# Six small experts of a mixture of experts: three products of 32 to 56 columns instead of two with high and low halves side by side, and one bias operation less

## The chip, the core and the metric

The kernel runs on one core of a Trainium2 chip. The metric is the device time of one execution in microseconds (us). The engines are named as in the profile: PE (TensorE, matrix products; PEld is its weight load), DVE (VectorE), ACT (ScalarE), POOL (GpSimd) and SP (SyncE, which here only issues transfers).

## The reference

One layer of a diffusion trunk on 1024 tokens of width 1024: a token-mixing half (windowed attention and a long convolution) and then a mixture of experts, the only part that the change touches. Cut to what matters:

```python
logits = xt @ router_w + router_b              # 1024 tokens, 32 experts
top_vals, top_idx = lax.top_k(logits, 4)
gate = jax.nn.softmax(top_vals, axis=-1)
# for every expert e, on the tokens tok that chose it, with their gates wt
hb = x[tok] @ w1[e] + b1[e]                    # 1024 -> 2048
glu, lin = jnp.split(hb, 2, axis=-1)
glu = jnp.minimum(glu, 7.0); lin = jnp.clip(lin, -7.0, 7.0)
act = glu * jax.nn.sigmoid(1.702 * glu) * (lin + 1.0)
yb = act @ w2[e] + b2[e]                       # 1024 -> 1024
acc = acc.at[tok].add(yb * wt[:, None])
```

All is float32, and each expert has 12 MB of weights.

## The kernel before

**Precision.** A float32 product is made of float16 ones: each operand is split into a high and a low half, and three passes are added in PSUM: high weight by high value, high weight by low value, low weight by high value. The weights of the experts come from HBM as float32 in 384 pieces of 1 MB (`raw`, line 305, five buffers). Each piece is split in two halves of 128x1024: ACT makes the high half `wh` (line 315) and DVE the low half `wl` (line 317).

**Experts by size.** The experts are sorted by how many tokens chose them, and the expert of rank r gets a fixed number of columns, `CAPS[r]`: 416, 384, 304, 256 and so on down to 56, 48, 32, 32, 32, 32. An expert is worked off in eight units. Units 0 to 3 take two pieces of w1 each (gate and linear part) and make 256 columns of the hidden layer, units 4 to 7 take one piece of w2 each.

**Order of the experts.** `plan` (line 74) interleaves two lanes: lane 0 takes the experts from the largest downward, lane 1 from the smallest upward. At each step it compares two running sums, the estimated product time and the estimated transfer time, and takes the next unit from lane 0 when products are not ahead by more than `SLACK`, else from lane 1. The estimate of an expert's product time is `pecost` (line 72). The framework's scheduler then sets the order on each engine from the program so written.

**Ahead of an expert** its tokens are fetched (`prep_`): DVE makes one-hot tables `S` (line 254), PE multiplies them with the token table (line 262, the index product), DVE turns the result into addresses (`gi`, line 264), POOL issues an indirect transfer that gathers up to 128 rows of 4 KB (line 277), and PE transposes the rows (line 286), which ACT copies to `xT` (line 287).

**Small experts before.** Experts with `C<=CCAT`, that is 56, 48 and four times 32 columns, take another way through `mm3`: their high and low values lie side by side, so that one product of 2C columns with the high weight does the first two passes, and a second of C columns with the low weight adds the third:

```python
if C<=CCAT:
    nc.tensor.matmul(ps_,wh,x[k],start=k==0,stop=False); nc.tensor.matmul(ps_[:,0],wl,x[k][:,0],start=False,stop=k==7)
    continue
for a,b in ((wh,x[0][k]),(wh,x[1][k]),(wl,x[0][k])):
    nc.tensor.matmul(ps_,a,b,start=n==0,stop=n==23); n+=1
```

The sum then lies in PSUM in two parts, and DVE adds them: with four operations more in a unit of w1 (line 396) and two more for each of the eight output blocks (line 420).

**Biases.** The 24 rows of biases of an expert are transposed by PE (line 364) and taken from PSUM by three small DVE operations (lines 366 to 368), which scale the two halves of b1 by 64, add 64 to the second one, and multiply b2 with the output gate.

Of the kernel before, what the change touches and what calls it, by code (L numbers as in the profile page):

```python
# [13 lines left out]
F32 = mybir.dt.float32  # L14
# [5 lines left out]
ALU = mybir.AluOpType  # L20
# [45 lines left out]
D=1024; T=1024; NE=32; NT=8  # L66
CAPS=[416,384,304,256,240,208,200,192,168,152,152,144,144,128,120,120,112,112,112,104,96,88,80,80,72,64,56,48,32,32,32,32]
DMAC,FLOOR,SLACK,PE0=33.7,22.0,10.0,10.0
CCAT=56
HOLD=[]; LMAX=152; HQ=1  # L70
def mmc(N): return max(FLOOR,0.4217*N+2.3)
def pecost(C): return (0.192*(mmc(2*C)+mmc(C)) if C<=CCAT else 0.576*mmc(C))+2.0*-(-C//128)
def dmacost(C): return DMAC+2.1*-(-C//128)
# [21 lines left out]
class Moe:  # L95
    def __init__(s,nc,tc,A,rows,accD,es):
        s.nc,s.tc,s.A,s.rows,s.accD,s.es=nc,tc,A,rows,accD,es
        s.cp=es.enter_context(tc.tile_pool(name="mc",bufs=1))
        nc,cp=s.nc,s.cp
        s.idf=cp.tile([128,128],F32,name="idf"); make_identity(nc,s.idf)  # L100
        s.idh=cp.tile([128,128],F16,name="idh"); nc.vector.tensor_copy(s.idh,s.idf)
        jp=cp.tile([128,128],I32,name="jp"); nc.gpsimd.iota(jp,pattern=[[1,128]],base=0,channel_multiplier=-1)
        s.tri=cp.tile([128,128],F16,name="tri"); nc.vector.tensor_scalar(s.tri,jp,0.0,None,op0=ALU.is_gt)
        s.ones=cp.tile([128,128],F16,name="ones"); nc.vector.memset(s.ones,1.0)
        s.iof=cp.tile([128,NE],F32,name="iof"); nc.gpsimd.iota(s.iof,pattern=[[1,NE]],base=0,channel_multiplier=0,allow_small_or_imprecise_dtypes=True)
        s.io16=cp.tile([128,512],F16,name="io16"); nc.gpsimd.iota(s.io16,pattern=[[1,512]],base=0,channel_multiplier=0,allow_small_or_imprecise_dtypes=True)
        s.pcol=cp.tile([128,1],F32,name="pcol"); nc.gpsimd.iota(s.pcol,pattern=[[0,1]],base=0,channel_multiplier=1,allow_small_or_imprecise_dtypes=True)
        s.dum=cp.tile([128,2],F32,name="dum")
        nc.vector.tensor_scalar(s.dum[:,0:1],s.pcol,1024.0,None,op0=ALU.add)
        nc.vector.tensor_scalar(s.dum[:,1:2],s.pcol,-1.0,-1024.0,op0=ALU.mult,op1=ALU.add)  # L110
        s.mx=cp.tile([128,NT,8],F32,name="mx"); s.mi=cp.tile([128,NT,8],U32,name="mi")
        s.oh=cp.tile([128,NT,4,NE],F16,name="oh"); s.idx=cp.tile([128,NT,4],F32,name="ridx"); s.A16=cp.tile([128,NT,NE],F16,name="A16")
        s.M=cp.tile([128,NT,NE,4],F16,name="M")
# [225 lines left out]
    def mm3(s,ps_,w,c,x,C):  # L339
        nc=s.nc; n=0  # L340
        for k in range(8):
            wh=w[0][:,k,c*128:(c+1)*128]; wl=w[1][:,k,c*128:(c+1)*128]
            if C<=CCAT:
                nc.tensor.matmul(ps_,wh,x[k],start=k==0,stop=False); nc.tensor.matmul(ps_[:,0],wl,x[k][:,0],start=False,stop=k==7)  # L344
# [12 lines left out]
    def expert_(s,C,p,reg,xT,chunks):  # L357
        nc,wk,ps,A=s.nc,s.wk,s.ps,s.A
        e=reg()
        T=lambda dt,name,bufs: wk.tile([128,PMAX[p]],dt,name=name+str(p),bufs=bufs)[:,:C]  # L360
        br=s.brs.pop(reg,None)
        if br is None: br=s.bias_load(e)
        pb=ps.tile([128,512],F32,name="tp",bufs=2)[:,:24]
        nc.tensor.transpose(pb,br,s.idf[:24,:24])
        bc=wk.tile([128,24],F32,name="bc",bufs=4)
        nc.vector.tensor_scalar(bc[:,0:8],pb[:,0:8],64.0,None,op0=ALU.mult)
        nc.vector.tensor_scalar(bc[:,8:16],pb[:,8:16],64.0,64.0,op0=ALU.mult,op1=ALU.add)
        nc.vector.tensor_tensor(bc[:,16:24],pb[:,16:24],s.g2c,op=ALU.mult)
        cat=C<=CCAT
        x=[xT[:,:,k,:C] for k in range(8)] if cat else [[xT[:,q,k,:C] for k in range(8)] for q in range(2)]  # L370
        ah,al=[],[]
        for u in range(4):

            wg=s.jget(); wl=s.jget()
            nb=2 if C<=256 else 1
            for c0 in range(0,2,nb):
                if cat:
                    t=ps.tile([128,4,2,64],F32,name="acc",bufs=4); pg,pl=t[:,0:2,:,:C],t[:,2:4,:,:C]
                elif C<=128:
                    t=ps.tile([128,4,128],F32,name="acc",bufs=4); pg,pl=t[:,0:2,:C],t[:,2:4,:C]  # L380
                else:
                    pg=ps.tile([128,nb,512//nb],F32,name="acc",bufs=4)[:,:,:C]; pl=ps.tile([128,nb,512//nb],F32,name="acc",bufs=4)[:,:,:C]
                for j in range(nb): s.mm3(pg[:,j],wg,c0+j,x,C)
                for j in range(nb): s.mm3(pl[:,j],wl,c0+j,x,C)
                if c0+nb==2: s.jahead(s.ahead)
                T2=lambda dt,name,bufs: wk.tile([128,max(2*PMAX[p],4*CCAT) if PMAX[p]<=256 else 512],dt,name=name+str(p),bufs=bufs)[:,:nb*C].rearrange("p (j c) -> p j c",j=nb)
                g=T2(F32,"sg",2); l=T2(F32,"sl",2); sg=T2(F32,"ss",1)
                for j in range(nb):
                    f=u*2+c0+j
                    if cat:  # L390
                        nc.vector.tensor_scalar(g[:,j],pg[:,j,0],bc[:,f:f+1],None,op0=ALU.add); nc.vector.tensor_scalar(l[:,j],pl[:,j,0],bc[:,8+f:9+f],None,op0=ALU.add)
                        continue
                    nc.vector.tensor_scalar(g[:,j],pg[:,j],bc[:,f:f+1],448.0,op0=ALU.add,op1=ALU.min)  # L393
                    nc.vector.tensor_scalar(l[:,j],pl[:,j],bc[:,8+f:9+f],512.0,op0=ALU.add,op1=ALU.min)  # L394
                if cat:
                    nc.vector.tensor_tensor(g,g,pg[:,:,1],op=ALU.add); nc.vector.tensor_scalar(g,g,448.0,None,op0=ALU.min); nc.vector.tensor_tensor(l,l,pl[:,:,1],op=ALU.add); nc.vector.tensor_scalar(l,l,512.0,None,op0=ALU.min)
                nc.scalar.activation(sg,g,AF.Silu,scale=1.702/64)
                nc.vector.scalar_tensor_tensor(l,l,-384.0,sg,op0=ALU.max,op1=ALU.mult)
                if cat:
                    hl=wk.tile([128,max(2*min(PMAX[p],256),4*CCAT)],F16,name="ah%d"%p,bufs=s.nact(p,nb))[:,:4*C].rearrange("p (j q c) -> p j q c",j=2,q=2); h,lo=hl[:,:,0],hl[:,:,1]  # L400
                else: h=T2(F16,"ah",s.nact(p,nb)); lo=T2(F16,"al",s.nact(p,nb))
                nc.scalar.activation(h,l,AF.Copy,scale=HSC)
                nc.vector.scalar_tensor_tensor(lo,l,HSC,h,op0=ALU.mult,op1=ALU.subtract)  # L403
                for j in range(nb):
                    if cat: ah.append(hl[:,j])
                    else: ah.append(h[:,j]); al.append(lo[:,j])
            yield
        yT=[]
        for u in range(4):

            w=s.jget()
            for c in range(2):
                m=u*2+c
                py=ps.tile([128,512],F32,name="acc",bufs=4)
                py=py[:,:2*C].rearrange("p (q c) -> p q c",q=2) if cat else py[:,:C]
                s.mm3(py,w,c,ah if cat else (ah,al),C)
                if c==1: s.jahead(s.ahead)
                y=T(F32,"yT",8)
                if cat:
                    nc.vector.tensor_copy(y,py[:,0]); nc.vector.tensor_tensor(y,y,py[:,1],op=ALU.add); py=y  # L420
                nc.scalar.activation(y,py,AF.Identity,bias=bc[:,16+m:17+m],scale=s.g2s[:,m:m+1])  # L421
                yT.append(y)
            yield
        s.tail.append(s.rows_out(C,chunks,yT))
        yield
# [943 lines left out]
```

## Time and profile before

| what | value |
|---|---|
| median of 3 runs | 2408.18 us (2398.25 to 2410.37) |
| the profiled execution's own time | 2412.69 us |
| its span in the trace | 2410.9 us |
| PE busy in the span | 2199.2 us (91%) |
| DVE busy in the span | 2053.8 us (85%) |
| ACT busy in the span | 1399.8 us (58%) |
| moved by DMA | 594.17 MB, mean 246 GB/s |

The experts fill the time from about 1047 us to about 2347 us. Shares are averages over the whole execution; the first part of the span is another computation with other limits. Durations of PE's products overlap, since they are pipelined: the pace of a run of products is read from the chain of waits, where a piece stands with its count and its length. The same holds for short DVE operations: the next one starts before the one ahead of it has ended.

### The profile page before, as it was taken

The page shows a single profiled execution, that of the slowest core. Times are in us where ns is not written, and L with a number is a line of the kernel's source. Part 1 is how long each engine was busy: PE and PEld are TensorE (multiplying, and loading weights), DVE is VectorE, ACT ScalarE, POOL GpSimd, SP SyncE. Part 2 cuts the span into 40 slices and gives each one's busy share as a digit, 9 for nine tenths or more (in the row PEclk, how much of TensorE's full clock was granted, in tenths as well). Part 3 has the DMA queues.
Part 4 walks back from the last instruction along what each step waited for, and adds up shares of the span by engine and source line. Part 5 has one row for each costly group of instructions (what it writes and reads, how often), then busy time and mean ns, then how long its engine had stood idle before and what let it go on. Part 6 is the DMA issues. An engine that isn't in the chain of part 4 may idle for free.

```text
span 2410.9 us, 59658 instructions
## 1 busy us (share of the span) xinstructions
PE 2199.2 (91%) x24732; PEld 1659.4 (69%) x24753; DVE 2053.8 (85%) x3767; ACT 1399.8 (58%) x2069; POOL 287.6 (12%) x176
## 2 busy tenths in 40 slices
PE   6899989999898999669999999998989999999991
PEld 4566565545454544346666778997989999999991
DVE  6776898798768858969989999988999999999985
ACT  3522335222236411356877778886878878788881
POOL 0000001000000000002031311212030221211110
PEclk9899999999779999779999999999999999999995
DMA  9424644555314233288999999999999999999984
GB/s 300 127 97 166 194 149 132 170 181 169 94 18 144 84 121 139 89 275 280 337 316 303 328 323 348 356 352 320 333 332 350 359 351 354 351 356 368 360 273 159
DMA packets 520011, 594.17 MB, mean 246 GB/s; under 512 B 16708, under 2 KB 472332, under 8 KB 519350
## 3 DMA queue, kind: packets, MB, share of 16 engines
q1 hardware_dynamic: 493048, 508.27, 62.6%
q0 software_dynamic: 13152, 43.69, 7.1%
q10 hardware_dynamic: 13534, 38.35, 4.7%
q8 instruction: 195, 3.19, 0.5%
q14 instruction: 82, 0.67, 0.1%
HBM read 532.95 MB, written 57.29 MB: 245 GB/s over the span
## 4 chain that ended last, share of the span: by engine, by line
PE 72%; DVE 15%; DMA 6%; ACT 3%; issue 3%; SPq 1%; DVEq 0%; ACTq 0%; POOLq 0%
PE acc L347 38%; PE mm L812 10%; DVE wl L317 4%; PE mm L1080 4%; PE mm L1121 3%; DVE bf L722 2%; PE ff L704 2%; DMA raw<-in_exp_w 2%; PE acc L344 2%; PE mm L975 2%; PE yt L433 1%; ACT wh L315 1%; DMA g<-rows,gi 1%; PE ff L899 1%; PE mm L572 1%
## 5 line engine op out<-in xcount | busy, mean ns | idle before, releaser
L317 DVE SCALAR_TENSOR_TENSOR wl<-raw,wh 128x1024 f16<-128x1024 f32 x768 | 906.0, 1215 | 56.2 <-ACT wh L315 52.7
L315 ACT ACTIVATE wh<-raw 128x1024 f16<-128x1024 f32 x768 | 769.9, 1050 | 181.7 <-PE acc L347 92.6
L347 PEld LDWEIGHTS <-wh 128*128 128x128 f16 x9984 | 778.2, 99 | 85.8 <-issue 12.9
L347 PE MATMUL acc<-xT,wh 128*128 128x80 f16 (+18 forms) x6656 | 717.3, 235 | 2.9 <-ACT wh L315 1.2
L347 PE MATMUL acc<-xT,wl 128*128 128x112 f16 (+19 forms) x3328 | 638.0, 235 | 2.3 <-DVE wl L317 2.3
L347 PEld LDWEIGHTS <-wl 128*128 128x128 f16 x4992 | 488.9, 98 | 45.7 <-issue 7.2
L347 PE MATMUL acc<-ah,wh 128*128 128x112 f16 (+19 forms) x1664 | 323.9, 236 | 6.0 <-ACT yT L421 3.0
L812 PE MATMUL mm<-hx,wh 128*128 128x512 f16 (+1 forms) x1072 | 322.7, 378 | 6.7 <-DVE hx L635 5.9
L347 PE MATMUL acc<-al,wh 128*128 128x112 f16 (+19 forms) x1664 | 323.3, 236 | 3.7 <-DVE al L403 3.7
L347 PE MATMUL acc<-ah,wl 128*128 128x112 f16 (+19 forms) x1664 | 322.3, 236 | 0.0
L812 PE MATMUL mm<-hx,wl 128*128 128x512 f16 x536 | 202.8, 378 | 0.0
L277 POOL DMA_INDIRECT g<-rows,gi x44 | 139.2, 3165 | 459.5 <-DVE tf L266 435.4
L436 POOL DMA_INDIRECT accD<-yr,si x49 | 115.9, 2366 | 617.2 <-ACT yr L435 383.3
L812 PEld LDWEIGHTS <-wh 128*128 128x128 f16 x1072 | 105.2, 98 | 118.8 <-issue 2.9
L722 DVE TENSOR_TENSOR bf<-bf 128x256 f32<-128x256 f32 (+1 forms) x272 | 131.2, 541 | 0.3
L421 ACT ACTIVATE yT<-acc,bc,g2s 128x112 f32<-128x112 f32 (+19 forms) x208 | 98.8, 484 | 25.7 <-PE acc L347 25.6
L812 PEld LDWEIGHTS <-wl 128*128 128x128 f16 x536 | 52.5, 98 | 66.4 <-issue 8.5
L394 DVE TENSOR_SCALAR sl<-acc,bc 128x112 f32<-128x112 f32 (+19 forms) x208 | 75.3, 377 | 14.8 <-PE acc L347 14.5
L344 PEld LDWEIGHTS <-wl 128*128 128x128 f16 x1152 | 78.2, 98 | 11.3 <-issue 8.8
L393 DVE TENSOR_SCALAR sg<-acc,bc 128x112 f32<-128x112 f32 (+19 forms) x208 | 75.3, 377 | 12.4 <-PE acc L347 12.2
L344 PEld LDWEIGHTS <-wh 128*128 128x128 f16 x1152 | 79.6, 102 | 4.0 <-DVE yT L420 2.1
L791 ACT ACTIVATE wh<-wr 128x1024 f16<-128x1024 f32 (+1 forms) x49 | 38.4, 813 | 72.0 <-PE mm L812 51.7
(379 smaller groups left out, 3409.0 us busy)
## 6 DMA issues: line engine op xcount, KB each, us to landing
raw<-in_exp_w SPq DMA_DIRECT2D x384, 1024.0 KB
wr<-in_w_in SPq DMA_DIRECT2D x34, 512.0 KB
t<-in_w_mod ACTq DMA_DIRECT2D x32, 512.0 KB
bf<-in_dec SPq DMA_DIRECT2D x32, 256.0 KB
Hd<-bf ACTq DMA_DIRECT2D x32, 256.0 KB
bf<-Hd SPq DMA_DIRECT2D x32, 256.0 KB
Gd<-t ACTq DMA_DIRECT2D x16, 512.0 KB
gt<-Gd SPq DMA_DIRECT2D x32, 256.0 KB
```

The source lines that it names most:

```text
L277: nc.gpsimd.indirect_dma_start(out=g[:cs].rearrange("p a d -> p (a d)"),out_offset=None,in_=s.rows,in_offset=bass.IndirectOffsetOnAxis(ap= ...
L315: else: nc.scalar.activation(wh[:,o],raw[:,o],AF.Copy,scale=sc)
L317: else: nc.vector.scalar_tensor_tensor(wl[:,o],raw[:,o],64.0,wh[:,o],op0=ALU.mult,op1=ALU.subtract)
L344: nc.tensor.matmul(ps_,wh,x[k],start=k==0,stop=False); nc.tensor.matmul(ps_[:,0],wl,x[k][:,0],start=False,stop=k==7)
L347: nc.tensor.matmul(ps_,a,b,start=n==0,stop=n==23); n+=1
L393: nc.vector.tensor_scalar(g[:,j],pg[:,j],bc[:,f:f+1],448.0,op0=ALU.add,op1=ALU.min)
L394: nc.vector.tensor_scalar(l[:,j],pl[:,j],bc[:,8+f:9+f],512.0,op0=ALU.add,op1=ALU.min)
L421: nc.scalar.activation(y,py,AF.Identity,bias=bc[:,16+m:17+m],scale=s.g2s[:,m:m+1])
L436: st=nc.gpsimd.indirect_dma_start(out=s.accD,out_offset=bass.IndirectOffsetOnAxis(ap=si[:cs,:1],axis=0),in_=yr[:cs],in_offset=None,compute ...
L722: (nc.gpsimd if pool and s.usepool else nc.vector).tensor_tensor(o,a,b,op=op)
L812: nc.tensor.matmul(p,w[a][:,k,:],s.hx[b][:,k,o],start=i==0,stop=i==23); i+=1
L1080: nc.tensor.matmul(p,w[a_][:,k,m*128:(m+1)*128],X[x][:,k,o] if b==0 else X[x][:,k,:],start=n==0,stop=n==11); n+=1
```

## The change

`CCAT` becomes 0, so that no expert is small enough for the side-by-side way. The estimates of `plan` see another price for the six experts, and the two lanes interleave in another order from the thirteenth unit on. The two DVE operations on b1 become one over 16 columns, with a constant table `bof` that is written once at the start.

```diff
-CCAT=56
+CCAT=0
 HOLD=[]; LMAX=152; HQ=1
 def mmc(N): return max(FLOOR,0.4217*N+2.3)
 def pecost(C): return (0.192*(mmc(2*C)+mmc(C)) if C<=CCAT else 0.576*mmc(C))+2.0*-(-C//128)
...
+        s.bof=cp.tile([128,16],F32,name="bof"); nc.vector.memset(s.bof[:,0:8],0.0); nc.vector.memset(s.bof[:,8:16],64.0)
...
         bc=wk.tile([128,24],F32,name="bc",bufs=4)
-        nc.vector.tensor_scalar(bc[:,0:8],pb[:,0:8],64.0,None,op0=ALU.mult)
-        nc.vector.tensor_scalar(bc[:,8:16],pb[:,8:16],64.0,64.0,op0=ALU.mult,op1=ALU.add)
+        nc.vector.scalar_tensor_tensor(bc[:,0:16],pb[:,0:16],64.0,s.bof,op0=ALU.mult,op1=ALU.add)
         nc.vector.tensor_tensor(bc[:,16:24],pb[:,16:24],s.g2c,op=ALU.mult)
```

Lines 108 to 365 have numbers higher by one after the change (346 and 347 become 347 and 348); from line 368 on they keep theirs.

On PE, at the first unit of the first expert with 32 columns, these rows stood before (`wh` and `wl` are the two halves of the weights, `xT` the values; 2x32 is high and low side by side):

```order
L364 MATMUL tp<-idf,br 128x24
L344 LDWEIGHTS wh
L344 MATMUL acc<-xT_10210,wh 128x2x32
L344 LDWEIGHTS wl
L344 MATMUL acc<-xT_10210,wl 128x32
```

and these stand there now:

```order
L365 MATMUL tp<-idf,br 128x24
L348 LDWEIGHTS wh
L348 MATMUL acc<-xT_10213,wh 128x32
L348 LDWEIGHTS wh
L348 MATMUL acc<-xT_10213,wh 128x32
L348 LDWEIGHTS wl
L348 MATMUL acc<-xT_10213,wl 128x32
```

For each of the eight blocks of 128 in depth, two products with two weight loads have become three with three.

On DVE, behind that same first unit, these rows stood before (`acc` is the PSUM result, `sg` and `sl` are the gate and the linear part; the rows at L204 and L207 belong to the gates of the tokens):

```order
L391 TENSOR_SCALAR sg_10579<-acc,bc 128x32
L391 TENSOR_SCALAR sl_10580<-acc,bc 128x32
L391 TENSOR_SCALAR sg_10579<-acc,bc 128x32
L391 TENSOR_SCALAR sl_10580<-acc,bc 128x32
L204 COPY ptt<-tp 128x128 x2
L317 SCALAR_TENSOR_TENSOR wl<-raw,wh 128x1024 x2
L396 TENSOR_TENSOR sg_10579<-sg_10579,acc 128x64
L396 TENSOR_TENSOR sl_10580<-sl_10580,acc 128x64
...
L396 TENSOR_SCALAR sg_10579<-sg_10579 128x64
L396 TENSOR_SCALAR sl_10580<-sl_10580 128x64
```

and these stand there now:

```order
L393 TENSOR_SCALAR sg_10612<-acc,bc 128x32
L394 TENSOR_SCALAR sl_10613<-acc,bc 128x32
L393 TENSOR_SCALAR sg_10612<-acc,bc 128x32
L394 TENSOR_SCALAR sl_10613<-acc,bc 128x32
L205 COPY ptt<-tp 128x128 x2
L318 SCALAR_TENSOR_TENSOR wl<-raw,wh 128x1024 x2
```

Four operations on 64 elements are gone from the unit; the four that read PSUM stay and take the clamp with them.

On PE, further on, the other interleaving puts the transposes of a gathered chunk at another distance from the index product that its gather waits for. For the first expert of 80 columns these rows stood before (`S` is its one-hot table, `g_18538` its gathered rows):

```order
L262 MATMUL tp<-M,S_18393 80x4
...
L286 LDWEIGHTS g_18538
L286 MATMUL tp<-idh,g_18538 128x80
```

and these stand there now, with all kinds of products that lie in between:

```order
L263 MATMUL tp<-M,S_19056 80x4
L365 MATMUL tp<-idf,br 128x24
L348 LDWEIGHTS wh
L348 MATMUL acc<-ah_18357,wh 128x304
...
L348 MATMUL acc<-al_18484,wh 128x64
L348 LDWEIGHTS wl
L348 MATMUL acc<-ah_18483,wl 128x64
L287 LDWEIGHTS g_19283
L287 MATMUL tp<-idh,g_19283 128x80
```

Between the index product and the transposes, where 168 products of experts stood, 42 stand now, six of them with 304 columns and 36 with 64.

## Rows read from the trace of the kernel before

**Rows 1.** The page, parts 1, 2 and 4: busy times, slices, the chain's shares.
```profile
PE 2199.2 (91%) x24732; PEld 1659.4 (69%) x24753; DVE 2053.8 (85%) x3767; ACT 1399.8 (58%) x2069; POOL 287.6 (12%) x176
...
PE 72%; DVE 15%; DMA 6%; ACT 3%; issue 3%; SPq 1%; DVEq 0%; ACTq 0%; POOLq 0%
```
**Rows 2.** Busy time by stage, experts only: stretch, length, each engine, clock, DMA.
```profile
core 0: us, PE busy (x) PEld busy (x) DVE busy (x) ACT busy (x) POOL busy (x), PEclk, DMA share, GB/s
1066.40:1432.00 365.60, 340.08 (x4179) 243.29 (x4179) 344.44 (x745) 272.42 (x392) 78.93 (x27) 0.94 0.96 315
1432.00:1600.00 168.00, 165.50 (x2711) 149.35 (x2710) 154.17 (x242) 142.20 (x198) 25.91 (x10) 1.00 1.03 347
1600.00:1800.00 200.00, 183.35 (x2914) 177.16 (x2912) 178.70 (x292) 151.83 (x205) 51.96 (x16) 0.97 1.02 330
2000.00:2200.00 200.00, 197.45 (x3227) 195.10 (x3225) 188.25 (x303) 169.88 (x233) 42.55 (x15) 1.00 1.07 359
2200.00:2347.00 147.00, 147.00 (x2381) 145.50 (x2379) 137.91 (x203) 123.86 (x169) 18.40 (x9) 1.00 1.00 334
```
**Rows 3.** The same view, two pieces of the first stage.
```profile
1066.40:1116.00 49.60, 45.66 (x516) 29.73 (x516) 49.31 (x114) 28.35 (x40) 5.64 (x2) 0.93 0.81 269
1116.00:1167.00 51.00, 44.75 (x658) 31.28 (x656) 50.69 (x113) 42.52 (x60) 14.36 (x4) 0.97 0.96 316
```
**Rows 4.** The chain of waits, clean pieces of PE: start, length, count of products.
```profile
1187.78 8.45 PE acc L347 x48
1196.23 1.73 PE acc L344 x64
...
1320.34 2.16 PE acc L344 x64
...
1378.71 2.40 PE acc L344 x64
...
1426.38 12.57 PE acc L347 x96
...
1439.40 1.39 PE acc L347 x47
```
**Rows 5.** Line 344: duration in ns (min/median/max), first and last start.
```profile
L344 PEld LDWEIGHTS <-wh x1152: 95/96/155, 1066.6 to 1424.6; 128*128 128x128 f16 x192
L344 PEld LDWEIGHTS <-wl x1152: 95/96/151, 1066.6 to 1424.7; 128*128 128x128 f16 x192
```
**Rows 6.** Groups of instructions: count, busy us, mean ns, idle time before.
```profile
L391 DVE TENSOR_SCALAR sg<-acc,bc 128x32 f32<-128x32 f32 (+2 forms) x48 | 11.8, 246 | 1.2 <-PE acc L344 1.2
...
L420 DVE COPY yT<-acc 128x32 f32<-128x32 f32 (+2 forms) x48 | 8.5, 189 | 6.7 <-PE acc L344 5.8 <-PE tp L364 0.8
L420 DVE TENSOR_TENSOR yT<-yT,acc 128x32 f32<-128x32 f32 (+2 forms) x48 | 8.1, 182 | 0.0
...
L396 DVE TENSOR_TENSOR sl<-sl,acc 128x64 f32<-128x64 f32 (+2 forms) x24 | 5.3, 223 | 0.0
L396 DVE TENSOR_TENSOR sg<-sg,acc 128x64 f32<-128x64 f32 (+2 forms) x24 | 5.3, 222 | 0.0
L366 DVE TENSOR_SCALAR bc<-tp 128x8 f32<-128x8 f32 x32 | 5.0, 156 | 10.6 <-PE tp L364 10.5
...
L396 DVE TENSOR_SCALAR sg<-sg 128x64 f32<-128x64 f32 (+2 forms) x24 | 4.5, 189 | 0.0
L396 DVE TENSOR_SCALAR sl<-sl 128x64 f32<-128x64 f32 (+2 forms) x24 | 4.5, 189 | 0.0
```
**Rows 7.** DVE in order of time: start, length, operation.
```profile
1188.85 0.21 DVE L396 TENSOR_TENSOR sg<-sg,acc 128x64 f32<-128x64 f32 x1
1188.97 0.24 DVE L391 TENSOR_SCALAR sl<-acc,bc 128x32 f32<-128x32 f32 x1
...
1230.55 0.28 DVE L420 COPY yT<-acc 128x32 f32<-128x32 f32 x2
1230.75 1.21 DVE L317 SCALAR_TENSOR_TENSOR wl<-raw,wh 128x1024 f16<-128x1024 f32 x1
...
1232.08 0.15 DVE L366 TENSOR_SCALAR bc<-tp 128x8 f32<-128x8 f32 x1
1232.15 0.15 DVE L367 TENSOR_SCALAR bc<-tp 128x8 f32<-128x8 f32 x1
```
**Rows 8.** PE in order of time: two index products, the transposes of their chunks.
```profile
1664.76 0.49 PE L262 MATMUL tp<-M,S 128*96 128x4 f16 x8
...
1677.48 1.46 PE L286 MATMUL tp<-idh,g 96*128 96x96 f16 x16 [7.07 <-DMA g<-rows,gi]
...
1794.47 0.73 PE L262 MATMUL tp<-M,S 128*112 128x4 f16 x16
1803.07 0.96 PE L286 MATMUL tp<-idh,g 112*128 112x112 f16 x16 [0.61 <-DMA g<-rows,gi]
```
**Rows 9.** Busy time around that first wait, columns as in rows 2.
```profile
1640.00:1660.00 20.00, 18.68 (x295) 17.87 (x294) 20.00 (x36) 13.55 (x18) 4.73 (x2) 1.00 1.07 344
...
1680.00:1740.00 60.00, 60.00 (x913) 58.38 (x912) 49.34 (x69) 46.55 (x64) 4.68 (x3) 0.97 0.94 306
```

## The prediction

> **What bounds the kernel now.** I read the shares of the engines first, then stages, because an average hides them. Over the whole span PE is busy 91%, and the chain of waits gives it 72% [rows 1]; DVE follows with 15%. By stage it looks different [rows 2]. From 2000 us on, PE is full: 197.45 of 200 us, then 147.00 of 147, at the full clock. From 1066 to 1432 us, the stage in which all six small experts run beside the three largest, it is not: PE is busy 340.08 of 365.6 us at a mean granted clock of 0.94, DVE 344.44. So in this stage DVE is a little ahead. In its first 100 us DVE is busy 49.31 of 49.60 and 50.69 of 51.00 us, all but without a pause, while PE stands at 92% and 88% [rows 3]. DVE makes the low halves of the weights, so when it is late, PE waits for weights. The reader is to see two engines that both nearly fill this stage, with DVE in front.
>
> How much must PE do there? Busy time at a clock of 0.94 is worth 340.08 x 0.94 = 319.7 us at the full clock. By the same product 1432 to 1600 us is worth 165.5 us of 168.
>
> **The third product.** An expert has 24 output blocks (four units of four, four units of two) and eight depths, so 192 places where two products become three. In clean pieces of the chain 64 products of the 32-column experts, half with 64 columns and half with 32, take 1.73 us, 27 ns each and 54 ns a pair [rows 4]. At 48 columns the 64 take 2.16 us (67.5 ns a pair), at 56 columns 2.40 us (75 ns a pair). The large experts pay by the column: 48 products of 416 columns take 8.45 us, 176 ns each, 0.42 ns a column. By that rate 64 and 32 columns would take 41 ns. They take 54, so a product of 32 columns costs about as much as one of 64, some 27 ns. Three of them are 81 ns. The added time is 27 ns x 192 = 5.2 us for each of the four experts of 32, 13.5 ns x 192 = 2.6 us for 48, and 6 ns x 192 = 1.2 us for 56: **24.5 us** in all. Upper bound: 47 products of 64 columns in another expert took 1.39 us, 29.6 ns each; by that it is 33 us. Lower bound, by the column alone: 13.5 ns x 192 x 4 = 10 us, which the pair of 54 ns speaks against.
>
> The Trainium skill has the same floor (TensorE: Matmul & The Clock Gate, section "Wait — 56ns, not 53.3ns?"): from the start of one product to the next never less than about 25 ns, however few the columns, with 32 columns as the example. It speaks against this change, since a third small product then costs a full place. By its 25 ns the estimate for the four experts of 32 would be 16 us instead of 20.7; the rows decide for 27.
>
> **What DVE gives back.** Line 396 goes: 4 operations in 24 units, 96 in all, 19.6 us by the busy times of the four groups. Line 420 goes: 96 operations, 8.5 + 8.1 = 16.6 us [rows 6]. Together 36.2 us. But short operations overlap: one of line 396 starts at 1188.85 and the next operation at 1188.97, 0.12 us later, where it itself lasts 0.21; two of line 420 start at 1230.55 and what follows at 1230.75, 0.10 us each [rows 7]. By this pace it is 96 x 0.12 + 96 x 0.10 = 21 us. I take 21, nearest to what DVE would have free, and keep 36 as the bound. The reads of PSUM change from line 391 (246 ns) to lines 393 and 394 with the same elements and one operation more inside; the low half is made by line 403 as before. I cost both at nothing.
>
> **What the stage makes of it.** PE's need goes from 319.7 to 344.2 us, DVE's from 344.4 to 323.4. The two change places. The fuller one fills as much of 365.6 us as before, and I expect the stage to stay as long: **0 us**. That is what hides the 24.5 us: time in which PE waited for DVE. Bounds: if PE fills the stage as it does at the end (147 of 147 [rows 2]), the stage is 344 us long, -21; if nothing is hidden, +24.5.
>
> **The biases.** 32 experts, one operation less each. Lines 366 and 367 start 0.07 us apart, last 0.15 us and have a mean of 156 ns [rows 6, 7]: 32 x 0.07 to 32 x 0.156, 2.2 to 5 us of DVE. PE is the bound in most stages, so I take **-2 us**, bounds 0 and -5. The two writes of `bof` stand once at the start, under 0.5 us by the same 0.15 us, while the first loads run.
>
> **The other order.** Nothing is computed more or less by it, but transposes move toward the index products of their gathers. From the end of an index product to the transposes it took 1677.48 - 1665.25 = 12.2 us in one case, where PE stood idle 7.07 us, and 1803.07 - 1795.20 = 7.9 us in another, with 0.61 us idle just ahead [rows 8]. PE has something to do in between only if products stand there. Counted in the order at the pace of rows 4, two chunks had less than 8 us of products before (4.1 and 5.0); now five have (1.7, 2.0, 4.4, 4.9, 7.1). At a mean of 10 us a gather, the shortfalls sum to 10.9 us before and 29.9 now, +19. With 7.9 us it is +12.5, with 12.2 us +25. Part of such a wait is not lost: ahead of the first one DVE was busy 20 of 20 us, behind it only 49.34 of 60, while PE ran without a pause [rows 9]; DVE and the loads had caught up. I take a third, **+6 us**; bounds 0 and +25. Behind the waiting transposes PE's whole queue stands, and then ACT's copies to `xT`.
>
> **The sum.** 2412.7 (the execution's own time) + 0 - 2 + 6 = 2416.7 us. The median of the runs shown is 2408.18, 0.2% below the profiled execution; on that scale it is **2412 us**, +0.2%.
>
> **Rivals.** *DVE was the only bound.* PE then fills the stage as at the end: -21, biases -2, gathers 0: 2390 in the profile's time, 2385 as a median; halfway 2395. For it: DVE's 99% in the first 100 us [rows 3]. Against: PE is at 93% over the stage, and its share grows.
>
> *PE was the bound already* (the other side). Between 1187 and 1208 us small and large units alternate, with no gap between 8.45 and 1.73 us pieces [rows 4]; there each small unit gets longer in full. If the whole stage is like that, +24.5 - 2 + 6: 2441, 2436 as a median. It decides once half of the 24.5 is uncovered. Against: DVE's lead in the stage.
>
> *Gathers come late at all five places*, and nothing is made up: 0 - 2 + 25: 2436, 2431 as a median. For it: 7.07 us idle in rows 8. It decides above 14 us.
>
> *Weight loads don't overlap at this size.* A load lasts 96 ns [rows 5], and 1152 more of them, one after the other, would be 110 us: about 2515. Against: 27 ns a product with its load in rows 4, where 64 loads are inside 1.73 us. The Trainium skill has such a price for streams of load and product (same page, section "Back-to-back issue gap"): about 81 ns a product at 128 columns. By this estimate 1152 products cost 93 us. The trace disagrees at these sizes.
>
> That the change does not do what it says is excluded: the order shows three products and no line 344.
>
> **Chances.** Forecast, within 0.5% (12 us, about what a measurement of this kernel can tell from no change): 0.50. DVE the only bound: 0.21. PE the bound: 0.18. Gathers: 0.09. Loads: 0.02. Faster by over 0.5% 0.21, slower 0.29. The range reaches from nearly the whole of the first rival, 2389, to the second, 2437.
>
> **What would show it.** Line 348 alone in the small experts, 64 products of 32 columns in 1.73 us, so 2.6 us for the 96 of a w1 unit. In the stage of the small experts DVE some 20 us less busy, PE over 95% of it, the stage as long as before within 10 us. More idle time of line 287 behind gathers than the 7.7 us in rows 8. Wrong if the stage is over 12 us longer or shorter, if DVE stays at 94% there, or if the time moves in a later stage, where nothing but the order has changed.

## The result and the profile after

The changed kernel takes **2481.27 us** (median of 4 runs, 2474.78 to 2498.26) against 2403.91 us before (4 runs, 2398.25 to 2410.37): ratio **1.0324**, 95% interval 1.0281 to 1.0367. The forecast was 2412 with a range of 2389 to 2437; the time lies 44 us above the range.

I begin with the page of the changed kernel (busy shares, DMA load and rate in 40 slices, the queue that carries the weights, the chain of waits):

```profile
PE 2238.8 (90%) x25904; PEld 1687.8 (68%) x25905; DVE 2036.6 (82%) x3545; ACT 1400.4 (56%) x2069; POOL 262.1 (10%) x176
...
DMA  9425644653304332579999999999999999999994
GB/s 289 132 85 185 197 133 144 177 182 133 76 30 153 102 112 110 168 244 319 330 321 284 305 298 318 331 274 339 329 331 326 312 333 317 338 336 339 346 287 154
...
q1 hardware_dynamic: 493048, 508.27, 64.2%
...
PE 28%; DMA 14%; DVE 5%; ACT 3%; issue 2%; DVEq 0%; ACTq 0%; POOLq 0%; SPq 0%
PE acc L348 26%; DMA raw<-in_exp_w 12%; DVE wl L318 2%; DMA g<-rows,gi 2%; ACT wh L316 2%; PE yt L433 1%; PE tp L287 1%; ACT xT L288 1%; DMA accD<-yr,si 0%; DVE ost L596 0%; DVE raw L1171 0%; DVE raw L1168 0%; DVE sg L393 0%; ACT yT L421 0%; PE tp L263 0%
```

The same two lines of the page of before:

```profile
GB/s 300 127 97 166 194 149 132 170 181 169 94 18 144 84 121 139 89 275 280 337 316 303 328 323 348 356 352 320 333 332 350 359 351 354 351 356 368 360 273 159
...
q1 hardware_dynamic: 493048, 508.27, 62.6%
```

The reader is to see one thing that no term of the prediction speaks of: the loads of the weights. The chain, of which PE had 72% and DMA 6% [rows 1], can after the change be followed back only to 1186 us, and in that half of the time `raw<-in_exp_w` alone takes 12% of the span, some 290 us. Twenty-two loads stand in it from 1602 us on, of 10 to 15 us each; over the whole span of before there were four, of 10 to 12 us. The DMA engines are as full as before (a 9 in each slice from the nineteenth to the thirty-ninth), but move 312 to 346 GB/s in most late slices where it was 350 to 368. The queue moves the same 508.27 MB in the same 493048 packets. Its time per MB follows from share times span over MB: 0.626 x 2410.9 / 508.27 = **2.97 us** before, 0.642 x 2496.5 / 508.27 = **3.15 us** after, +6%. The same bytes have become slower.

Where does the time lie? Cut at the last product of the small experts (line 344 before, 32 to 56 columns on line 348 after), the windows of before and then of after read so (window, its length, busy us of PE, PEld, DVE, ACT, POOL with instructions, granted clock, DMA share, GB/s):

```profile
1066.60:1424.90 358.30, 333.82 (x4132) 238.70 (x4132) 337.46 (x734) 267.56 (x384) 78.93 (x27) 0.94 0.96 315
1424.90:2357.10 932.20, 905.32 (x14569) 876.11 (x14567) 852.78 (x1334) 761.26 (x1040) 173.38 (x64) 0.99 1.03 341
```

```profile
1080.10:1437.40 357.30, 332.24 (x5168) 242.74 (x5168) 306.49 (x518) 261.23 (x377) 62.12 (x26) 0.94 0.98 305
1437.40:2442.90 1005.50, 934.49 (x14686) 900.30 (x14684) 866.75 (x1326) 768.01 (x1047) 164.56 (x66) 0.97 1.04 320
```

The stage of the small experts, the only one in which the change adds products, is as long as before: 357.3 against 358.3 us. The loss, 1005.5 - 932.2 = **73.3 us**, lies behind it. The work on the two sides of the cut is not quite the same: with 1152 products more before would have 5284 in the stage, and the changed kernel has 5168 there and 117 more than before behind it. The new order has moved some 116 products of other experts across the cut. The sum of the two windows has the same work in both kernels, and it went from 1290.5 to 1362.8 us, **72.3 us**. The other 13 us between the two profiled executions lie ahead of the small experts, which start at 1080.1 instead of 1066.6 us. They can't be put to the change: the first split of a weight starts at 1038.6 us here and at 1026.5 before, and at 1006 to 1029 in the runs that follow, whatever they change. This execution is also the slowest of the four.

PE is busy 29 us longer behind the cut (934.49 against 905.32). Some 117 products are only a part of that; the granted clock is the other. Cut into pieces of 20 us, the stretch behind the cut has it at 1.00 (the upper level, 2.4 GHz) in all but 4 of 47 pieces before and all but 11 of 51 after; in each of those PE had stood idle, in the piece itself or in the one ahead of it. PE's idle time there went from 26.9 to 71.0 us, and busy time x (1 - clock), an estimate of what the lower clock costs, from 6.1 to 23.7. So a wait is paid once in idle time, and part of it again in a lower clock. Line by line, what ACT's high halves (line 315 before, 316 after) sat idle for, before and then after:

```profile
L315 ACT ACTIVATE wh<-raw x768: 1038/1047/1112, 1026.5 to 2342.5; 128x1024 f16<-128x1024 f32 x192
...
  DMA raw<-in_exp_w: 46.9, 33
```

```profile
L316 ACT ACTIVATE wh<-raw x768: 1039/1049/1149, 1038.6 to 2428.4; 128x1024 f16<-128x1024 f32 x192
...
  DMA raw<-in_exp_w: 148.9, 108
```

The operation itself lasts the same 1.05 us; it waits 108 times for a load instead of 33 times. A piece of the chain of after, late in the run (start, length in us, what), shows how such a wait looks:

```profile
1918.50 1.74 DVE wl L318 x2
1920.23 0.54 issue
1920.77 0.11 DVE al L403
1920.88 14.01 DMA raw<-in_exp_w
...
1944.18 1.02 DVE wl L318
...
1946.61 14.47 DMA raw<-in_exp_w
...
1961.19 2.00 ACT wh L316 x2
```

The chain passes from DVE to the next load, the load takes 14 us, and the splits behind it have nothing to split. That DVE frees the load's buffer there is inferred; the rows name only the engine and the line.

A smaller second loss is in PE's list of waits (us in all, times, longest), before and then after:

```profile
PE tp L286 <- DMA g<-rows,gi: 10.2, 3, 7.1
```

```profile
PE tp L287 <- DMA g<-rows,gi: 28.3, 6, 11.0
PE acc L348 <- ACT ah L402: 26.9, 9, 8.7
```

The first line is the gathers. The second, 2.1 us in 2 waits before, goes with the loads: it is back at 2.4 us in `e3` below, which has the new order and `raw` at a multiple of 256 bytes. `ah` is ACT's work, as are the splits `wh` that wait for loads.

### The profile page after: what moved, and what is told of

Its sections match the earlier page's. It is cut to its first block, busy times and chain, and to the rows that moved or that the text cites. A ratio compares the mean times of both kernels' runs of the same rounds, so it can differ in the third digit from the quotient of the medians.

```text
span 2496.5 us, 61755 instructions
## 1 busy us (share of the span) xinstructions
PE 2238.8 (90%) x25904; PEld 1687.8 (68%) x25905; DVE 2036.6 (82%) x3545; ACT 1400.4 (56%) x2069; POOL 262.1 (10%) x176
## 3 DMA queue, kind: packets, MB, share of 16 engines
q1 hardware_dynamic: 493048, 508.27, 64.2%
## 4 chain that ended last, share of the span: by engine, by line
PE 28%; DMA 14%; DVE 5%; ACT 3%; issue 2%; DVEq 0%; ACTq 0%; POOLq 0%; SPq 0%
PE acc L348 26%; DMA raw<-in_exp_w 12%; DVE wl L318 2%; DMA g<-rows,gi 2%; ACT wh L316 2%; PE yt L433 1%; PE tp L287 1%; ACT xT L288 1%; DMA accD<-yr,si 0%; DVE ost L596 0%; DVE raw L1171 0%; DVE raw L1168 0%; DVE sg L393 0%; ACT yT L421 0%; PE tp L263 0%
## 5 line engine op out<-in xcount | busy, mean ns | idle before, releaser
L348 PE MATMUL acc<-xT,wh 128*128 128x32 f16 (+22 forms) x8192 | 781.5, 225 | 6.8 <-issue 6.1
L348 PE MATMUL acc<-xT,wl 128*128 128x32 f16 (+22 forms) x4096 | 702.3, 225 | 1.7 <-issue 1.7
L348 PE MATMUL acc<-ah,wh 128*128 128x32 f16 (+22 forms) x2048 | 364.0, 228 | 34.0 <-ACT ah L402 26.9
L348 PE MATMUL acc<-al,wh 128*128 128x32 f16 (+22 forms) x2048 | 363.6, 228 | 1.3 <-DVE al L403 1.3
L348 PE MATMUL acc<-ah,wl 128*128 128x32 f16 (+22 forms) x2048 | 362.0, 228 | 0.6 <-issue 0.6
L421 ACT ACTIVATE yT<-acc,bc,g2s 128x32 f32<-128x32 f32 (+22 forms) x256 | 118.2, 468 | 27.1 <-PE acc L348 27.0
L393 DVE TENSOR_SCALAR sg<-acc,bc 128x32 f32<-128x32 f32 (+21 forms) x256 | 87.4, 354 | 28.0 <-PE acc L348 27.6
L394 DVE TENSOR_SCALAR sl<-acc,bc 128x32 f32<-128x32 f32 (+21 forms) x256 | 87.2, 353 | 15.3 <-PE acc L348 15.1
L288 ACT ACTIVATE xT<-tp 128x1024 f16<-128x1024 f16 (+14 forms) x98 | 72.4, 777 | 22.9 <-PE tp L287 22.9
L287 PE MATMUL tp<-idh,g 128*128 128x128 f16 (+14 forms) x704 | 49.2, 220 | 37.4 <-DMA g<-rows,gi 28.3
```

Of the source, the lines that this page charges most:

```text
L287: for k in range(8): nc.tensor.transpose(pt[:,k],g[:cs,q,k*128:(k+1)*128],s.idh[:cs,:cs])
L288: nc.scalar.activation(st['x'][:,q,:,c0:c0+cs],pt,AF.Copy)
```

## The experiments

**Theory.** `bof` is a tile of 64 bytes a partition in the pool that is allocated first, so each later buffer lies 64 bytes further on. In the compiled kernels the five `raw` buffers begin at byte 29952 before (117 x 256) and at 30016 after (64 more than a multiple of 256), 8192 apart. *Theory A:* loads into a buffer off a multiple of 256 are slower. *Rival B:* the new order and the third product cost the time, through waits for gathers (2% in the chain of after). *Rival C:* an engine's operand at a shifted address is slower, whichever buffer it is. The first four runs, `e1` to `e4`, set A against B.

**The parts of the change apart.** `e1_ccat_only` is the kernel before with `CCAT=0`; `e2_bias_only` has only the edit of the biases with its `bof`; `e3_after_256` is the whole change with `bof` cut from a tile of 256 bytes.

```diff
# e3, against the changed kernel
-        s.bof=cp.tile([128,16],F32,name="bof"); nc.vector.memset(s.bof[:,0:8],0.0); ...
+        s.bof=cp.tile([128,64],F32,name="bof")[:,0:16]; nc.vector.memset(s.bof[:,0:8],0.0); ...
```

> The six small experts run three passes in the new order; biases keep their three operations, so that no table bof stands in SBUF and every buffer of the weights lies at the address that it had before (raw at 29952 + n x 8192 bytes of a partition). Theory of the address (the 64 bytes of bof shift all buffers behind it, and the transfers into them take longer): about 2412, as the prediction had it for three passes and order, without its 2 us for biases; the queue of the weights takes 3.0 us of 16 engines' time per MB. Theory of the third product and the new order (the prediction's rivals, larger than thought): about 2480, as the change.

> The bias edit alone, with its table bof of 64 bytes; the small experts run as before. raw lies 64 bytes higher than before, as in the change. Theory of the address: 2460 to 2485, with the queue of the weights at about 3.15 us of 16 engines' time per MB. Theory of the third product and the order: 2402 to 2406, a shade under before.

> The whole change, with bof held in a tile of 256 bytes of which 64 are used: raw lies 256 bytes higher than before, at multiples of 512. Theory of the address: about 2410, like the change without its loss, if what counts is the remainder by 256 or 512. Theory of the third product and the order: about 2480.

| run | us | ratio to before, 95% | queue, us per MB | PE's waits for gathers, us (times) |
|---|---|---|---|---|
| `e1_ccat_only` | 2419.49 | 1.0090 (1.0056 to 1.0123) | 2.98 | 25.8 (5) |
| `e2_bias_only` | 2466.25 | 1.0252 (1.0205 to 1.0299) | 3.16 | 9.9 (2) |
| `e3_after_256` | 2416.39 | 1.0061 (1.0038 to 1.0085) | 2.98 | 28.8 (6) |

The edit that removes 32 small operations costs 2.5%, and the same table in 256 bytes makes the loss vanish but for 0.6%. Two losses, then: one that hangs on 64 bytes, and one on `CCAT`. (A ratio is to the kernel before as it ran beside that run.)

**The 64 bytes.** `e4_pad64` is the kernel before with a tile of 64 bytes that nothing reads, in the place of `bof`. `e5_raw_only64` moves `raw` alone (64 bytes ahead of it, 448 behind), `e6_all_but_raw64` moves all buffers behind `raw`, but not `raw`. `e9_bias_256` is the edit of the biases with `bof` in 256 bytes.

```diff
# e4
+        s.pad=cp.tile([128,16],F32,name="pad"); nc.vector.memset(s.pad,0.0)
# e5: ahead of the first raw, and behind it
+        s.pre=s.ww.tile([128,16],F32,name="wpre"); nc.vector.memset(s.pre,0.0)
...
+        s.post=s.ww.tile([128,112],F32,name="wpost"); nc.vector.memset(s.post,0.0)
# e6: behind raw only
+        s.post=s.ww.tile([128,16],F32,name="wpost"); nc.vector.memset(s.post,0.0)
```

> The kernel before with nothing but a tile of 64 bytes, written once and never read, at the place of bof. Theory of the address: 2460 to 2485, the same as the bias edit alone. Theory of the third product and the order: 2404, as before.

> The kernel before, with a tile of 64 bytes ahead of the five raw buffers and one of 448 bytes behind them: only raw lies 64 bytes higher, wh, wl and all behind lie 512 bytes higher and keep their remainder by 512. Theory that the transfers into raw are slow at an address that is no multiple of 256: about 2459, as with the 64 bytes ahead of everything. Theory that the reads and writes of the engines, or the gathers, are what suffers: about 2400.

> The counterpart: raw stays where it was, wh, wl and all buffers of the experts behind them lie 64 bytes higher. Theory of the transfers into raw: about 2400. Theory of the engines or the gathers: about 2459.

> The bias edit alone, with bof in a tile of 256 bytes, so that raw lies at a multiple of 512. Theory of the address: 2400 to 2404, a thousandth under before or the same, since one short DVE operation less for each of 32 experts is 2 to 5 us of an engine that is not the bound in most stages. If something else in the edit cost time (the read of bof, the longer operation): over 2416.

| run | us | ratio to before, 95% | queue, us per MB |
|---|---|---|---|
| `e4_pad64` | 2459.16 | 1.0233 (1.0197 to 1.0269) | 3.16 |
| `e5_raw_only64` | 2463.09 | 1.0250 (1.0204 to 1.0295) | 3.14 |
| `e6_all_but_raw64` | 2402.97 | 0.9997 (0.9970 to 1.0025) | 2.97 |
| `e9_bias_256` | 2403.06 | 1.0001 (0.9977 to 1.0024) | 2.97 |

An unused tile does it, and it does it through `raw` alone: rival C falls with `e6`, in which every buffer behind `raw` is shifted, those of the gathers too, and no time is lost. What ACT's splits wait for loads separates all runs in the same way: 140 to 166 us in the changed kernel and the five runs with `raw` off a multiple of 256 (`e2`, `e4`, `e5`, and `e11` and `e12` below), 33 to 55 us in `e1`, `e3` and `e6` to `e10` and 46.9 before. The windows of `e4`, cut as above:

```profile
1058.40:1416.30 357.90, 332.69 (x4132) 238.02 (x4132) 337.56 (x732) 268.50 (x384) 76.96 (x27) 0.94 1.01 314
1416.30:2405.00 988.70, 926.41 (x14568) 894.06 (x14567) 857.70 (x1335) 761.90 (x1040) 166.40 (x64) 0.96 1.05 322
```

With two products, the old order and the old biases this gives 357.9 + 988.7 - 1290.5 = 56.1 of the 72.3 us, all of it behind the small experts.

**Which addresses.** The same unused tile with 128 and with 32 bytes puts `raw` at remainders of 128 and 32 by 256.

```diff
# e11, e12
+        s.pad=cp.tile([128,32],F32,name="pad"); nc.vector.memset(s.pad,0.0)
+        s.pad=cp.tile([128,8],F32,name="pad"); nc.vector.memset(s.pad,0.0)
```

> The kernel before with an unused tile of 128 bytes instead of 64: raw at a remainder of 384 by 512, a multiple of 128 and not of 256. If a multiple of 128 is enough: about 2402. If it takes 256: about 2460, or between, if the loss falls with the remainder.

> The same with 32 bytes: raw at a remainder of 288 by 512, a multiple of 32 and not of 64. If any remainder that is not a good one costs the same: about 2460. If the loss grows with a finer remainder: over 2480. If the case of 64 was a special one: about 2402.

2450.6 us, 1.0219 (1.0180 to 1.0257), and 2461.91 us, 1.0261 (1.0220 to 1.0302): the remainders 32, 64 and 128 are slow alike. By 512, `raw` lay at a remainder of 256 in the kernel before and of 0 in `e3`, and both are at 2.97 or 2.98 us per MB, so what counts of the addresses tried is 256.

**The other loss: third product or order.** `e7_3pass_oldplan` has three products in the old order, `e8_2pass_newplan` two products in the new order, both with the old biases.

```diff
# e7, against the kernel before
 PLAN=plan()
+CCAT=0
# e8, against the kernel before: CCAT is 0 only while plan runs
-CCAT=56
+CCAT=0
...
 PLAN=plan()
+CCAT=56
```

> No table bof, addresses as before. The two lanes interleave as before, with the old prices, and the small experts run three passes: the third product and the saved DVE operations without the new order. Theory that the new order costs what is left of the loss: 2395 to 2405. Theory that the third product costs it: about 2419, as with both.

> The counterpart, addresses as before: the new order with high and low halves side by side, so no third product. Theory that the new order costs what is left: 2410 to 2420. Theory of the third product: about 2400.

2407.38 us, 1.0015 (0.9992 to 1.0039), and 2404.11 us, 0.9991 (0.9967 to 1.0015). Neither costs anything alone; PE's waits for gathers are 9.4 us in `e7` and 10.8 in `e8`, as before (10.2). Only both together give 25.8 and 28.8. Windows of `e7` and then of `e3`, cut as above:

```profile
1048.10:1407.60 359.50, 340.22 (x5271) 248.09 (x5271) 315.19 (x540) 264.75 (x382) 81.05 (x26) 0.96 0.95 310
1407.60:2340.10 932.50, 911.00 (x14583) 882.87 (x14580) 853.83 (x1335) 763.69 (x1042) 197.69 (x65) 0.99 1.03 342
```

```profile
1063.80:1417.90 354.10, 330.47 (x5167) 239.65 (x5167) 305.89 (x518) 260.37 (x377) 64.42 (x25) 0.96 0.94 308
1417.90:2371.50 953.60, 918.29 (x14687) 886.98 (x14684) 863.25 (x1326) 766.48 (x1047) 180.61 (x66) 0.99 1.02 337
```

In `e7` both stretches are as long as before. In `e3`, which like the change has some 116 products on the other side of the cut, the two together take 1307.7 us, 17.2 more than before. (`e7`'s profiled execution is the fastest of its ten, `e3`'s the slowest of its six; the ratios have all of them.) To see whether it is the gathers, `e10_early_gather` takes `e3` and starts the one-hot table, the index product and the gather of each expert but the first pair one unit earlier, and the transposes of experts of one or two chunks one unit later:

```diff
# e10, against e3
-        steps[1].append(one)
-        for i in range(n if G0 is not None else min(n,2)): steps[2+min(i,1)].append(lambda i=i: gather(i))
-        t0=4 if n>2 else 5
+        steps[1 if G0 is not None else 0].append(one)
+        for i in range(n if G0 is not None else min(n,2)): steps[(2 if G0 is not None else 1)+min(i,1)].append(lambda i=i: gather(i))
+        t0=4 if n>2 else (5 if G0 is not None else 6)
```

> The whole change with bof in 256 bytes, and in the preparation of an expert the one-hot table and the gather stand one unit earlier, the transposes of one or two chunks one unit later. By the order no gather then has less than 6.9 us of products between its index product and its transposes (1.7, 2.0, 4.4 and 4.9 in the change). Theory that the waits for gathers are what the three passes in the new order still cost: these waits fall from 28.8 to under 12 us, and the time from 2416 to 2396 to 2405. Theory that it is the third product: the waits fall and the time stays at about 2416.

2400.85 us, 0.9993 (0.9965 to 1.0021), with 12.4 us of waits for gathers in 2 places, and the two windows together at 1292.3 us. The 0.6% is gone, with the third product and the new order still in. Neither `e10` nor `e9` is faster than the kernel before beyond its interval; no run found a version that is. The early gathers were not tried on the kernel before.

**Why the loads are slow.** The last six runs ask whether the transfer is slow by itself or only beside engines that use SBUF. They hold the 384 loads of 1 MB, with `raw` at a multiple of 256 and at 64 more, without and with the splits.

```diff
# e13, e14 (pad of 704 bytes instead of 640), e17 (768)
+        pad=wp.tile([128,160],F32,name="pad"); nc.vector.memset(pad,0.0)
+        for e in range(NE):
+            for u in range(12):
+                W,o=(A['exp_w1'],u*256) if u<8 else (A['exp_w2'],(u-8)*256)
+                raw=ww.tile([128,8,256],F32,name="raw",bufs=5)
+                nc.sync.dma_start(raw,W[e].rearrange("(k p) f -> p k f",p=128)[:,:,o:o+256])
...
# e15 and e16 (704 bytes) add, for both halves h of raw
+                    nc.scalar.activation(wh[:,h],raw[:,h],AF.Copy,scale=64.0)
+                    nc.vector.scalar_tensor_tensor(wl[:,h],raw[:,h],64.0,wh[:,h],op0=ALU.mult,op1=ALU.subtract)
```

> This kernel leaves out everything but 384 loads of 1 MB of the experts' weights into five buffers raw, whose addresses are a multiple of 256, and a write of the last buffer to the output. No engine reads what is loaded. Nothing but transfers bounds it: 402.7 MB at the 2.97 us a MB that the queue took in the kernel before would be 1196 us, at the 369 GB/s of its last stage 1091 us. Both theories expect 1090 to 1200 us; it is the measure for the next run.

> The same loads alone, the buffers 64 bytes further on (remainder 64 by 256). If the transfer into such an address is slower by itself: longer than the run before by 4 to 6%, since the queue's time a MB went from 2.97 to 3.15 us with the change. If it is slow only beside engines that read and write SBUF: the same time within 0.5%.

> The 384 loads and the splits of every piece by ACT and DVE, as in the kernel before, no products; raw at a multiple of 256. DVE needs 768 x 1.2 us = 922 us, less than the loads, so the loads bound it: as long as the loads alone, 1090 to 1200 us, by the theory that the write alone matters; if engines' accesses slow the transfers, some per cent longer than the loads alone.

> Loads and splits, raw (and the halves behind it) 64 bytes further on. If the write is slow by itself: the same 4 to 6% over the run before as without the splits. If it takes engines beside it: 4 to 6% here and nothing in the loads alone. If it takes the products too: nothing in either pair.

| run | us (range of 4 runs) |
|---|---|
| `e13_loads_256` | 1061.62 (1061.58 to 1061.73) |
| `e14_loads_64` | 1175.66 (1175.56 to 1175.71) |
| `e15_split_256` | 1067.25 (1067.14 to 1067.31) |
| `e16_split_64` | 1180.58 (1180.50 to 1180.64) |

The pages of `e13` and of `e14` (DMA load and rate in 40 slices):

```profile
DMA  9999999999999999999999999999999999999998
GB/s 349 386 386 386 386 386 386 386 386 386 386 386 386 386 386 386 386 386 386 386 386 386 386 386 386 386 386 386 386 386 386 386 386 386 386 386 386 386 386 340
```

```profile
DMA  9999999999999999999999999999999999999998
GB/s 321 348 348 348 348 348 348 348 348 348 348 348 348 348 348 348 348 348 348 348 348 348 348 348 348 348 348 348 348 348 348 348 348 348 348 348 348 348 348 313
```

386 against 348 GB/s, with no engine at work. The transfer itself is slower, and 1175.66 / 1061.62 is 10.7% more time. My 4 to 6% was too low. The splits add 5 to 6 us to either, 0.5%, so the difference doesn't come from contention with ACT and DVE.

Two more runs change the remainder to 128, and the rows from 1 KB to 4 KB (`raw` at 64 by 256):

```diff
# e18, against e14
-                nc.sync.dma_start(raw,W[e].rearrange("(k p) f -> p k f",p=128)[:,:,o:o+256])
+                a,c=((u//2)*256,(u%2)*1024) if u<8 else ((u-8)*256,0)
+                nc.sync.dma_start(raw.rearrange("p (k q) c -> p k (q c)",k=2),W[e].rearrange("(g k p) f -> g p k f",p=128,k=2)[a//256][:,:,c:c+1024])
```

> The loads alone again (all else is left out), raw at a remainder of 128 by 256. If a row that starts off a multiple of 256 costs one extra part whatever the remainder: as long as with a remainder of 64, 1176 us within 1%. If the cost grows with the remainder: twice the 114 us that a remainder of 64 added, about 1290 us. If 128 is aligned enough: 1062 us.

> The loads alone at a remainder of 64 by 256, but each 1 MB piece cut as 2 rows of 4 KB for each partition instead of 8 of 1 KB (the same bytes in all; the buffers' places unchanged). If each row that starts off a multiple costs a fixed extra: a quarter of the 114 us, about 1090 us. If the cost goes with the bytes: 1176 us. That aligned rows of 4 KB take about as long as aligned rows of 1 KB is assumed here and not measured.

1175.61 us (1175.48 to 1175.72) for `e17`, the same as with 64. 1004.34 us (1003.32 to 1005.61) for `e18`. So the price doesn't grow with the remainder between 64 and 128. Whether it goes by the row or by the byte stays open. `e18` was to tell the two apart, at 1090 or at 1176 us, and it met neither, because the assumption in it does not hold: even off a multiple, rows of 4 KB beat aligned rows of 1 KB. It takes aligned rows of 4 KB to decide, which were not run. Its page has a quarter of the packets:

```profile
GB/s 350 410 410 409 410 409 410 409 410 409 410 410 410 410 410 410 409 409 411 409 409 410 409 409 409 409 410 409 410 409 409 409 410 409 410 409 411 409 410 304
DMA packets 105603, 406.90 MB, mean 405 GB/s; under 512 B 6272, under 2 KB 6272, under 8 KB 105600
```

## Why the prediction was wrong

**The step that failed** is the last sentence on the biases: "The two writes of `bof` stand once at the start, under 0.5 us by the same 0.15 us, while the first loads run." I priced the instructions of the new tile and not its place. That missing term is 2.3 to 2.5% (`e4`, `e5`, `e2`), 56 to 61 us of 2404, and no rival had it. It is a cost put at nothing without a reason. The mechanism is shown from both ends: an unused tile brings the loss, `e3` and `e9` remove it, and the loads alone have it.

**Why 2.3% and not 10.7%.** The rate that the kernel needed says it. Loads off a multiple ran at 348 GB/s (`e14`), aligned at 386 (`e13`). The kernel shows nearly the same two limits, in the busiest of the pieces of 20 us behind the small experts, before and then after (columns as in rows 2):

```profile
1964.90:1984.90 20.00, 16.97 (x263) 16.62 (x261) 19.26 (x43) 13.70 (x20) 6.38 (x2) 0.97 1.08 386
```

```profile
2197.40:2217.40 20.00, 18.23 (x313) 17.96 (x311) 16.60 (x27) 15.01 (x23) 1.02 (x1) 1.00 1.08 352
```

In `e4` the busiest piece has 352 too, in `e3` some have 384 and 388. Before, 22 of the 47 pieces moved more than 352 GB/s; there, by these limits, loads off a multiple can't follow. In the stage of the small experts it is 2 of 18, and there `e4` lost nothing (357.9 us against 358.3). On average the kernel before moved 341 GB/s over the 932 us, which leaves a reserve of 12% to 386 and of 2% to 348, and 315 in the stage ahead of it, where 9% is left. The size is an estimate: at 352 GB/s the 22 pieces would take 20 us longer, and the lower clock behind the added waits costs `e4` 23 us (29.6 against 6.1, counted as above), together 43 of its 56 us. The rest stays open. The prediction read the DMA share of 1.07 in [rows 2] and gave it no term. Its own test named the symptom: wrong "if the time moves in a later stage, where nothing but the order has changed".

**The other order: +6 was mis-sized.** Measured is 0.6% (`e3`, with the third product and the biases in it), 0.0061 x 2404 = 15 us, interval 9 to 20. The gross estimate was right: +19 us of shortfalls, and PE's waits for gathers went from 10.2 to 28.8 us, +18.6. What failed is "I take a third": some four fifths of it was lost, half to all by the interval. The argument had been that behind one such wait DVE had caught up [rows 9]. `e10` confirms the cause, since gathers that start a unit earlier, with transposes a unit later, take the loss away. The estimate took the new order for the cause; `e8`, at 10.8 us of such waits, shows that it needs the third product as well. How the two together place the transposes so close was not followed up.

**The third product: right, 0 us in its stage.** In `e7`, where the order is the old one, the stage lasts 359.5 us against 358.3, and the two engines change places as told: DVE goes from 94.2% of it to 87.7%, PE from 93.2% to 94.6%. The size in it is not confirmed. PE's busy time x clock, the measure of the forecast, goes from 333.82 x 0.94 = 313.8 to 340.22 x 0.96 = 326.6 us, 13 more and not 24.5, so some luck may be in the 0. The pace was as predicted, 27 ns a product at 32 columns: one piece of the chain of after has 120, all of 32 columns, in 3.15 us, 26 ns each.

```profile
1193.14 3.15 PE acc L348 x120
```

**DVE's gain: right.** From 337.46 to 315.19 us in `e7`, -22.3 where 21 stood; the 734 operations became 540, 194 fewer where 192 were foreseen. One sign failed, if narrowly: PE's share was to pass 95%, and is 94.6% in `e7` and 93.0% in the changed kernel, which has fewer products in that stage. What keeps the stage as long, with neither engine full, was not tried apart.

**The biases: -2 can't be told from 0.** `e9` gives 1.0001, interval 0.9977 to 1.0024, that is -6 to +6 us.

**The rivals.** "DVE was the only bound" and "PE was the bound already" both fall with `e7`, at +1.2 us in the stage. "Gathers come late at all five places" is the one that happened in part: `e3` runs at 2416 us (beside 2399 for the kernel before), between the forecast and that rival's 2431. "Weight loads don't overlap" falls by the 26 ns. With the address mended the time lies in the range and near the forecast.

**The parts add up.** 2.3% for the address (`e4`) and 0.6% for the gathers (`e3`) make 2.9%, within the errors of the 3.2% measured; in the two windows 56.1 + 17.2 = 73.3 us, against 72.3. Single executions of one kernel differ by 10 to 30 us, so that the second agreement is closer than it had to be.

## What to carry to other kernels

A new tile, however small, can move every buffer that is allocated after it: compare the addresses of the buffers that large transfers write to in both builds, and keep them at multiples of 256 bytes, above all where the loads run near their limit. Rows of 1 KB are the case that was measured here. Price a change by what it moves as well as by what it issues, and give a term to each resource that has no reserve in its stage, even one that the change doesn't seem to touch. And take a wait that you counted at its full price, unless a row shows that it is made up.

## What the hardware showed

**The address that a transfer writes.** 384 MB in rows of 1 KB took 1061.62 us into buffers at a multiple of 256 bytes, and 1175.66 and 1175.61 us at 64 and 128 bytes more. That is 114 us for 384 x 1024 rows on 16 engines, 114 x 16 / 393216 = 4.6 ns for each row of 1 KB, on 43.2 ns. The Trainium skill (DMA: Bandwidth & Descriptors, section "How a descriptor splits into AXI transactions") has a rule of this kind: a piece that starts off a multiple of 256 B is cut at the multiples, which makes an estimate of five transactions and not four for 1 KB, with 34 beats of 32 B at a remainder of 64 and 36 at 128, where 32 would do. The equal times at 64 and 128 agree with its transactions and not with its beats. The size, 10.7%, fits neither: 5/4 would be 25%, 34/32 and 36/32 6% and 12.5%. The Trainium skill tells it of what a transaction reads; in these runs the address read stayed, and only the address written changed.

**The length of a row.** Rows of 4 KB came at 409 to 411 GB/s off a multiple, faster than aligned rows of 1 KB at 386. What aligned rows of 4 KB reach was not measured, and neither was a kernel that cuts the weights so: its pieces would hold 256 rows of the weight over 1024 columns instead of 1024 rows over 256, and the order of the products would have to follow.
